# Modulation sums by transposes and ScalarE row sums in the first stage of a decoder layer

## The chip, the cores and the metric

The kernel runs on one NeuronCore of one Trainium2 chip. The metric is device time in microseconds for one execution of the whole program; before the change it is 685.23 us, the median of 3 runs (684.47 to 685.48).

## The reference, cut to what matters

One decoder layer over 512 tokens of width 1024. The part that the change touches is its beginning: the modulation vector from the condition `c`, the modulated RMSNorm and the first columns of the input projection.

```python
cs = jax.nn.silu(c)
mod = cs @ w_ada[l] + b_ada[l]
shift1, scale1, gate1, shift2, scale2, gate2 = [m[:, None, :] for m in jnp.split(mod, 6, axis=-1)]
h = _rmsnorm(x, norm1_g[l]) * (1.0 + scale1) + shift1
proj = h @ w_in[l]
qa, ka, va, qd, kd, vd, ga, gd = jnp.split(proj, points, axis=-1)
...
return _rmsnorm(x, final_g)
```

Behind it come sliding-window attention, differential attention, gates, an output projection and a gated MLP with a convolution; none of that is changed.

## The kernel before, in words

The first stage works on the 1024 channels in eight blocks of 128, k = 0 to 7. For each k it needs `mods[k]`, two numbers per channel: a scale (column 0) and a shift (column 1). With them ScalarE makes `hTh[k]`, the transposed, normalised and modulated activations (128 channels by 512 tokens), and a plain copy `hf`, from which VectorE makes the remainder `hTl[k]`: an fp32 operand is carried as a high and a low part, and a product takes three matrix products (high by high, high by low, low by high). The 768 columns of this stage's projection (queries, keys and values of the first branch) lie in six PSUM banks, `acc6`, which take the products of all eight k. `DONE = (0, 4, 2, 5, 1, 3)` (line 175) is the order of the banks; the sixth is bank 3.

TensorE's work on one k is written out in `mm_k` (line 396): part 0 is high by high and high by low over the banks, twelve products of 512 columns; part 2 is the six products with `hTl[k]`. In the loop over `gi` (line 484) the modulation sums of the next k stand between the two. They are made as follows.

- `ac_first` and `ac_ops` (lines 282 and 292): `w_ada`'s block for k (`adaw`, two halves, j = 0 for scale and 1 for shift) has 1024 rows, eight groups of 128. ScalarE multiplies two of the groups by silu(c), VectorE adds the other six (`scalar_tensor_tensor`, line 301) and folds the two partial sums into one tile `ac[k][0]` (line 302), 128 partitions by two times 128 columns. What is left is a sum over the 128 partitions.
- `reduce_mod` (line 317) makes that sum on TensorE: for each j a product of `ac` with one column of ones (line 328), which leaves 128 x 1 numbers in the PSUM tile `pa`.
- `finish_mod` (line 331): VectorE computes (pa + bsc1) * n1g into column 0 (line 334), ScalarE pa + bsh into column 1 (line 338).
- `h_turn` (line 376) transposes the next block of the normalised input, `xt`, four transposes; `h_tile` (line 381) is the two ScalarE passes to `hTh` and `hf` (line 384).

k = 0 and k = 1 have paths of their own (`direct0`, `early_mod`), which the change leaves alone. The order of VectorE, ScalarE and TensorE in this stage is that of the code (`manual_schedule`); the loads stand on SyncE's queue in the order `adaw`, `w0` for k = 0 to 7 (lines 243 to 250). Behind the loop a scheduler places the next stage's instructions, some of them among the last ones of this stage: the casts `w768_0_h` and `w1280_0_h` of the next stage's weights (line 128) on ScalarE, their remainders (line 129) on VectorE, and `pcv`, a small transpose of convolution constants (line 561), with its copy `cv` (line 563).

A step is named by its `gi` below: step gi multiplies block gi and prepares block gi + 1, so the changed steps are 1 to 6.

Of the kernel before, what the change touches and what calls it, by code (L numbers as in the profile page):

```python
# [8 lines left out]
F32 = mybir.dt.float32  # L9
F32R = mybir.dt.float32r  # L10
AF = mybir.ActivationFunctionType
ALU = mybir.AluOpType
PSUM = bass.MemoryType.PSUM

P = 128
# [45 lines left out]
def kernel(  # L61
# [22 lines left out]
    nc = tc.nc  # L84
# [3 lines left out]
    def pool(name, bufs=1, space=None, stack=ctx):  # L88
        kw = {} if space is None else {"space": space}
        return stack.enter_context(tc.tile_pool(name=name, bufs=bufs, reuse_waits="tile", **kw))  # L90

    cpool = pool("const")
# [13 lines left out]
    def tbank(name, shape=(P, S)):  # L106
        return bank("t", 2, list(shape), name)
# [34 lines left out]
    ones = cpool.tile([P, P], F32, name="ones")  # L142
    nc.gpsimd.memset(ones, 1.0)
    ident = cpool.tile([P, P], F32, name="ident")
# [31 lines left out]
    DONE = (0, 4, 2, 5, 1, 3)  # L176
# [42 lines left out]
    pp = pool("p1", stack=p1)  # L219
# [54 lines left out]
    cols = cpool.tile([P, NR], F32, name="cols")  # L274
    nc.vector.tensor_copy(cols, pc)
    bsh, bsc1, n1g, sublnc = cols[:, 0:8], cols[:, 8:16], cols[:, 16:24], cols[:, 24:25]
    nc.vector.tensor_scalar_add(bsc1, bsc1, 1.0)
    nc.vector.tensor_scalar_mul(n1g, n1g, -0.5)
    nc.vector.tensor_scalar_mul(sublnc, sublnc, -0.5 * (1.0 - LAM_INIT))
    ac, mods, wts = {}, {}, {}  # L280


    def ac_first(gi, b):
        a = pp.tile([P, 2, P], F32, tag=f"ac{b}", bufs=2, name=f"ac{gi}_{b}")
        aw = adaw[gi]
        if gi < ALONE and b:
            nc.vector.tensor_scalar_mul(a, aw[:, :, b], cs[:, b : b + 1])
        else:
            nc.scalar.activation(a, aw[:, :, b], AF.Copy, scale=cs[:, b : b + 1])
        ac.setdefault(gi, {})[b] = a  # L290

    def ac_ops(gi, low):
        aw = adaw[gi]
        if gi < ALONE:
            ac_first(gi, 1)
        order = (3, 2, 5, 4) if gi == 1 else (3, 5, 2, 7, 4, 6) if gi < ALONE else (3, 2, 5, 4, 7, 6)
        for n, kk in enumerate(order):
            if gi == 1 and n == 1:
                split_lo(0, 1)
            a = ac[gi][kk % 2]  # L300
            nc.vector.scalar_tensor_tensor(a, aw[:, :, kk], cs[:, kk : kk + 1], a, ALU.mult, ALU.add)
        nc.vector.tensor_add(ac[gi][0], ac[gi][0], ac[gi][1])
        low()

    def direct(pa, j, k, kks, start=True, stop=False):
        for kk in kks:
            nc.tensor.matmul(
                pa[:, j],
                adaw[k][:, j, kk],
                cs[:, kk : kk + 1].to_broadcast([P, P]),  # L310
                start=start and kk == kks[0],
                stop=stop and kk == kks[-1],
            )

    def early_mod(gi):
        pa = tbank(f"pa{gi}", (P, 2, P))
        direct(pa, 0, gi, (6, 7))
        return pa

    def reduce_mod(gi, early=None):  # L320
        pa = early or tbank(f"pa{gi}", (P, 2, P))
        for j in range(2):
            if early:
                if j:
                    direct(pa, 1, gi, (6, 7))
                nc.tensor.matmul(pa[:, j], ac[gi][0][:, j], ones, start=False, stop=True)
            else:
                nc.tensor.matmul(pa[:, j, 0:1], ac[gi][0][:, j], ones[:, 0:1], start=True, stop=True)
        return pa

    def finish_mod(k, pa):
        pa = pa if k == 0 else [pa[:, 0], pa[:, 1]]
        m = pp.tile([P, 16], F32, tag="mod", bufs=3, name=f"mod{k}")
        last = nc.vector.scalar_tensor_tensor(
            m[:, 0:1], pa[0][:, 0:1], bsc1[:, k : k + 1], n1g[:, k : k + 1], ALU.add, ALU.mult
        )
        if k:
            nc.scalar.activation(m[:, 1:2], pa[1][:, 0:1], AF.Identity, bias=bsh[:, k : k + 1])
        else:
            nc.vector.tensor_add(m[:, 1:2], pa[1][:, 0:1], bsh[:, k : k + 1])  # L340
        mods[k] = m
        return last

    def w0_views(k):
        wh, wl = wts[k]
# [9 lines left out]
    def split_hi(k, part=None):  # L355
        if part != 1:
            pl, nb = (wp, WB) if k % 2 == 0 else (pp, 2)
            wh = pl.tile([P, 768], F32R, tag="whi", bufs=nb, name=f"w0h{k}")
            wl = pl.tile([P, 768], F32R, tag="wlo", bufs=nb, name=f"w0l{k}")
            wts[k] = (wh, wl)  # L360
            rq, wq, lq = w0_views(k)
            nc.scalar.copy(wq, rq)
        if part != 0:
            nc.scalar.copy(wts[k][0][:, 512:768], w0[k][:, 512:768])

    def split_lo(k, part):
        wh, wl = wts[k]
        if part == 0:
            rq, wq, lq = w0_views(k)
            nc.vector.tensor_tensor(lq, rq, wq.bitcast(F32), ALU.subtract)  # L370
        else:
            nc.vector.tensor_sub(wl[:, 512:768], w0[k][:, 512:768], wh[:, 512:768].bitcast(F32))
# [3 lines left out]
    def h_turn(k):  # L376
        pts[k] = tbank(f"xt{k}")
        for t in range(NT):
            nc.tensor.transpose(pts[k][:, t * P : (t + 1) * P], xn[:, t, k * P : (k + 1) * P], ident)

    def h_tile(k, between=None):
        hf = pp.tile([P, S], F32, tag="hf", bufs=2, name=f"hf{k}")
        for dst in (hTh[k], hf):
            nc.scalar.activation(dst, pts[k], AF.Identity, bias=mods[k][:, 1:2], scale=mods[k][:, 0:1])
            if dst is not hf and between is not None:
                between()
            if dst is not hf and k + 1 < ALONE:
                ac_first(k + 1, 0)
        hfs[k] = hf

    def h_low(k):
        nc.vector.tensor_sub(hTl[k], hfs[k], hTh[k].bitcast(F32))

    FIRST = (0, 2, 1, 3, 4, 5)

    def mm_k(k, part, some=DONE):
        wh, wl = wts[k]
        last = k == KT - 1
        if part == (2 if last else 1):
            return  # L400
        for i in some:
            for p in (1, 2) if last and part else (0, 1) if part == 0 and not last else (part,):
                lhs, rhs = ((wh, hTh), (wl, hTh), (wh, hTl))[p]
                nc.tensor.matmul(
                    acc6[i], lhs[:, i * P : (i + 1) * P], rhs[k], start=k == 0 and p == 0, stop=last and p == 2
                )
# [28 lines left out]
    def scale_x(t):  # L435
        nc.scalar.activation(xn[:, t, HEAD:], xn[:, t, HEAD:], AF.Copy, scale=rst[:, t : t + 1])
# [37 lines left out]
    for j in range(2):  # L474
        nc.tensor.matmul(pa0[j], a0[j], ones, start=False, stop=True)
    turn(3)
    finish_mod(0, pa0)
    split_hi(0, 0)
    keep_warm(2)
# [3 lines left out]
    for gi in range(KT):  # L483
        more = gi + 1 < KT
        if more:
            if gi == 0:
                scale_x(2)
            split_hi(gi + 1)
            if gi == 1:
                scale_x(3)  # L490
            ac_ops(gi + 1, lambda: h_low(gi))
        else:
            h_low(gi)
            lp = cpool.tile([P, 2, 64], F32, name="lp")
            ls = cpool.tile([P, 2], F32, name="ls")
            nlam = cpool.tile([P, 1], F32, name="nlam")
            nc.vector.tensor_mul(lp, lamv[:, 0:4:2], lamv[:, 1:4:2])
            nc.vector.reduce_sum(ls, lp, axis=mybir.AxisListType.X)
            nc.scalar.activation(ls, ls, AF.Exp)
            nsink = cpool.tile([P, 8], F32, name="nsink")  # L500
            nc.vector.tensor_scalar_mul(nsink, sink, -1.0)
            nc.vector.tensor_sub(nlam, ls[:, 1:2], ls[:, 0:1])
            nc.vector.tensor_scalar_add(nlam, nlam, -LAM_INIT)
        if gi == 0:
            h_turn(1)
        mm_k(gi, 0, DONE if gi else FIRST[:5])
        mm_k(gi, 1)
        if more:
            if gi == 0:
                split_lo(1, 0)  # L510
            pa = reduce_mod(gi + 1, early_mod(1) if gi == 0 else None)
            if gi == 0:
                mm_k(0, 0, FIRST[5:])
            if ALONE <= gi + 2 < KT:
                ac_first(gi + 2, 1)
                ac_first(gi + 2, 0)
            if gi:
                h_turn(gi + 1)
            last_mod = finish_mod(gi + 1, pa)
            if gi:  # L520
                split_lo(gi + 1, 0)
            split_lo(gi + 1, 1)
            h_tile(gi + 1)
        mm_k(gi, 2)
# [503 lines left out]
    for i in range(SWA_PAIRS):  # L1028
        more = i + 1 < SWA_PAIRS
# [502 lines left out]
    last = range(KT - TAIL, KT)  # L1532
# [568 lines left out]
```

## Time and profile before

| what | value |
|---|---|
| median of 3 runs | 685.23 us |
| the profiled execution's own time | 685.38 us |
| its span, first to last instruction | 683.6 us |
| TensorE busy in the span | 673.7 us (99%) |
| VectorE, ScalarE, GpSimd busy | 562.5, 398.1, 98.4 us |
| granted TensorE clock | 0.997 |

Times in rows are microseconds from the start of the span, and the second number of a timeline row is how long the instruction took. PE is TensorE's products, PEld its weight loads, DVE VectorE, ACT ScalarE, POOL GpSimd, SP the load queue. Products are pipelined, so a product's share of the time is the distance to the next one's start, not its length. An `x4` behind a row counts instructions that were merged. Names of tiles lose their numbers in the trace: `pa` is the modulation sums of any k.

### The profile page before, as it was taken

Reading aid. Unit: us, or ns where it says so; the run is one execution under the profiler, and the core shown is the slowest. Engines: PE = TensorE matmul, PEld = TensorE weight load, DVE = VectorE, ACT = ScalarE, POOL = GpSimd, SP = SyncE. Lnnn points to the kernel's source line nnn. Section 1 sums busy time; section 2 is a strip of 40 time slices with the busy share of each in tenths; the row PEclk is TensorE's granted clock in tenths of the full one; section 3 lists DMA queues with packets and bytes.
Section 4 is the critical chain, followed back from the end, with each engine's and each line's share of the span. In section 5 each row is a group of like instructions: output and inputs, shape, how many; then the busy total and the mean of one; then the engine's idle time right before and its main releaser. Section 6 shows DMA issues by size and latency. Waiting matters only on the chain. (4 is left out here: it accounts for less than half of the span.)

```text
span 683.6 us, 10903 instructions
## 1 busy us (share of the span) xinstructions
PE 673.7 (99%) x4005; PEld 582.2 (85%) x4005; DVE 562.5 (82%) x1075; ACT 398.1 (58%) x722; POOL 98.4 (14%) x119
## 2 busy tenths in 40 slices
PE   8999999999999999999999999999999999999995
PEld 5887887878888888888899999999999998888885
DVE  4999875988796756794589988988888999979997
ACT  6776774546543223233377756666666776656765
POOL 3000000011022011021030101112111102440300
PEclk9999999999999999999999999999999999999998
DMA  9995422565466885469644788886879848995903
GB/s 304 351 301 175 144 62 65 161 167 163 142 159 179 254 245 164 163 187 340 204 89 108 174 195 206 185 184 190 213 163 217 207 146 203 201 204 144 167 1 123
DMA packets 117141, 123.87 MB, mean 181 GB/s; under 512 B 5063, under 2 KB 94184, under 8 KB 117088
## 3 DMA queue, kind: packets, MB, share of 16 engines
q1 hardware_dynamic: 97246, 95.11, 44.2%
q0 software_dynamic: 19648, 27.79, 24.3%
q8 instruction: 31, 0.51, 0.3%
q10 hardware_dynamic: 194, 0.28, 0.1%
q14 instruction: 22, 0.18, 0.1%
HBM read 118.97 MB, written 2.11 MB: 177 GB/s over the span
## 5 line engine op out<-in xcount | busy, mean ns | idle before, releaser
L1390 PE MATMUL up<-t,m_whi 128*128 128x256 f32 x512 | 93.5, 283 | 0.1
L1390 PEld LDWEIGHTS up<-t,m_whi 128*128 128x128 f32 x512 | 79.8, 192 | 0.8 <-ACT up L1427 0.3
L1390 PE MATMUL up<-t,m_wlo 128*128 128x256 f32 x256 | 72.4, 283 | 0.0
L953 POOL DMA_DIRECT2D arow<-arow x28 | 22.5, 802 | 249.1 <-DVE sd L822 123.2
L1390 PEld LDWEIGHTS up<-t,m_wlo 128*128 128x128 f32 x256 | 49.1, 192 | 0.0
L1373 PE MATMUL up<-bhl,p_whi 128*128 128x512 f32 x136 | 48.9, 399 | 0.0
L1272 POOL DMA_DIRECT2D s<-in_w_up_dram x21 | 26.9, 1352 | 144.2 <-DMA s<-in_w_up_dram 65.8
L1302 ACT CAST m_whi<-s 128x1024 fp32r<-128x1024 f32 x31 | 32.6, 1052 | 23.8 <-PE up L1390 10.3
L1306 DVE TENSOR_TENSOR m_wlo<-s,m_whi 128x1024 fp32r<-128x1024 f32 x31 | 37.9, 1221 | 6.0 <-ACT m_whi L1302 5.5
L945 DVE SCALAR_TENSOR_TENSOR arow<-ra,cs,arow 128x512 f32<-128x512 f32 x56 | 41.7, 747 | 0.6
L1377 PE MATMUL up<-bhl,p_wlo 128*128 128x256 f32 x136 | 38.3, 281 | 0.0
L1390 PE MATMUL up<-bhl,p_whi 128*128 128x256 f32 x192 | 35.1, 283 | 0.0
L1390 PE MATMUL up<-t,p_whi 128*128 128x256 f32 x176 | 32.1, 283 | 0.0
L1373 PEld LDWEIGHTS up<-bhl,p_whi 128*128 128x128 f32 x136 | 25.6, 188 | 5.5
L1390 PEld LDWEIGHTS up<-bhl,p_whi 128*128 128x128 f32 x192 | 30.0, 192 | 0.0
L817 ACT ACTIVATE sd<-sd,dmx 128x128 f32<-128x128 f32 (+3 forms) x32 | 17.7, 556 | 17.2 <-DVE dmx L807 17.2
L1390 PEld LDWEIGHTS up<-t,p_whi 128*128 128x128 f32 x176 | 27.4, 191 | 0.4
L1390 PE MATMUL up<-bhl,p_wlo 128*128 128x256 f32 x96 | 27.2, 283 | 0.0
L1377 PEld LDWEIGHTS up<-bhl,p_wlo 128*128 128x128 f32 x136 | 25.7, 189 | 0.0
L1390 PE MATMUL up<-t,p_wlo 128*128 128x256 f32 x88 | 24.9, 283 | 0.0
L1296 DVE TENSOR_TENSOR s<-s,wa 128x1024 f32<-128x1024 f32 x20 | 24.4, 1219 | 0.0
L1397 ACT ACTIVATE gT<-a,cv 128x512 f32<-128x512 f32 x22 | 17.8, 814 | 10.1 <-DVE a L1431 6.2
(501 smaller groups left out, 2085.6 us busy)
## 6 DMA issues: line engine op xcount, KB each, us to landing
ra<-in_w_ada_dram SPq DMA_DIRECT2D x32, 512.0 KB, 4.5
wa<-in_w_up_dram SPq DMA_DIRECT2D x22, 512.0 KB, 4.6
s<-in_w_up_dram SPq DMA_DIRECT2D x21, 512.0 KB, 5.6
s<-in_w_up_dram POOLq DMA_DIRECT2D x21, 512.0 KB, 7.3
w<-in_w_in_dram SPq DMA_DIRECT2D x12, 512.0 KB, 4.8
a<-in_w_up_dram SPq DMA_DIRECT2D x11, 512.0 KB, 4.2
b<-in_w_down_dram SPq DMA_DIRECT2D x10, 512.0 KB, 3.9
adaw<-in_w_ada_dram SPq DMA_DIRECT2D x8, 512.0 KB, 6.8
```

Source lines behind the costliest of these rows:

```text
L817: exp = nc.scalar.activation(pm[m], pm[m], AF.Exp, bias=mx[:, m : m + 1], scale=slope, accum_out=ls)
L945: nc.vector.scalar_tensor_tensor(ac, r[:, a], cc, ac, ALU.mult, ALU.add)
L953: nc.gpsimd.dma_start(whole[0:n], whole[n : 2 * n], accum_op=ALU.add)
L1272: nc.gpsimd.dma_start(dst, upblock(*blk), accum_op=ALU.add)
L1296: nc.vector.tensor_add(src, src, R[J, "a11" if name == "m6" else "a12"])
L1302: nc.scalar.copy(W[J, name][0], R[J, SRC[name]])
L1306: nc.vector.tensor_sub(lo, R[J, SRC[name]], hi.bitcast(F32))
L1373: nc.tensor.matmul(bk, wh[:, k, cu], bhl[:, i, k].rearrange("p b n -> p (b n)"), start=False, stop=k == 3, skip_group_check=True,)
L1377: nc.tensor.matmul(bk[:, :H], wl[:, k, cu], bhl[:, i, k, 0], start=False, stop=k == 3, skip_group_check=True)
L1390: nc.tensor.matmul(o[u], w[:, k, cu], b[:, k], start=opens and k == 0 and x == 0, stop=k == 3 and x == 2, skip_group_check=True,)
L1397: nc.scalar.activation(grow(j), av[J][:, u], AF.Identity, bias=cv[:, 66 + j : 67 + j], scale=cv[:, 44 + j : 45 + j])
```

## The change

For k from 2 on, `reduce_mod` no longer multiplies `ac` by ones. It transposes both halves on TensorE, 128 x 128 each, so that the numbers to be added lie along a row. `finish_mod` then reads `pa` on ScalarE alone: an Identity activation over 128 columns with `accum_out`, which writes the row's sum into the column of `mods[k]`; scale and bias are applied to every element, so the bias is a 128th of what it was. These shares are made once, in step 1, in a new tile `share`: a ScalarE pass over 128 x 16 numbers and a GpSimd multiplication of 128 x 8. VectorE has no part left in it. The elements themselves go to a tile `spread`, which nobody reads.

The transposes also stand elsewhere: from step 1 on the six banks' first twelve products are cut into five banks, then the modulation, then the sixth bank.

```diff
-                nc.tensor.matmul(pa[:, j, 0:1], ac[gi][0][:, j], ones[:, 0:1], start=True, stop=True)
+                nc.tensor.transpose(pa[:, j], ac[gi][0][:, j], ident)
...
-        last = nc.vector.scalar_tensor_tensor(
+        if k > 1:
+            for j, scale, bias in ((0, n1g[:, k : k + 1], share[:, 8 + k : 9 + k]), (1, 1.0, share[:, k : k + 1])):
+                spread = pp.tile([P, P], F32, tag="spread", name=f"spread{k}_{j}")
+                last = nc.scalar.activation(spread, pa[j], AF.Identity, bias=bias, scale=scale, accum_out=m[:, j : j + 1])
+            mods[k] = m
+            return last
+        nc.vector.scalar_tensor_tensor(
...
+                nc.scalar.activation(share, cols[:, 0:16], AF.Copy, scale=1.0 / P)
+                nc.gpsimd.tensor_tensor(share[:, 8:16], share[:, 8:16], n1g, ALU.mult)
...
-        mm_k(gi, 0, DONE if gi else FIRST[:5])
+        mm_k(gi, 0, DONE[:5] if gi and more else DONE if gi else FIRST[:5])
...
-            if gi == 0:
-                mm_k(0, 0, FIRST[5:])
+            mm_k(gi, 0, (DONE if gi else FIRST)[5:])
```

On TensorE in step 1, before the change (`a1` is the fifth bank's sum, `a3` the sixth's, `w0h1` and `w0l1` the weights' two parts):

```order
L404 MATMUL a1_114<-hTA_116,w0h1_293 128x512
L404 MATMUL a1_114<-hTA_116,w0l1_294 128x512
L404 MATMUL a3_115<-hTA_116,w0h1_293 128x512
L404 MATMUL a3_115<-hTA_116,w0l1_294 128x512
L328 MATMUL pa2_373<-ones_67,ac2_0_337 128x1 x2
L379 MATMUL xt2_380<-ident_69,xn_122 128x128 x4
L404 MATMUL a0_110<-hTA_116,w0h1_293 128x512
```

The same place with the change:

```order
L410 MATMUL a1_114<-hTA_116,w0h1_294 128x512
L410 MATMUL a1_114<-hTA_116,w0l1_295 128x512
L329 MATMUL pa2_374<-ident_69,ac2_0_338 128x128 x2
L410 MATMUL a3_115<-hTA_116,w0h1_294 128x512
L410 MATMUL a3_115<-hTA_116,w0l1_295 128x512
L385 MATMUL xt2_383<-ident_69,xn_122 128x128 x4
L410 MATMUL a0_110<-hTA_116,w0h1_294 128x512
```

The pair on `ac2` stands two products of 512 columns earlier and is a pair of transposes; it is no longer next to the transposes of `xt2`. The other five steps read the same.

On ScalarE around the last block's modulation, before (`mod7` is `mods[7]`, `hThB` the last two blocks of `hTh`, the two `w..._h` the next stage's weights):

```order
L364 CAST w0h7_599<-w0_7_175 128x256
L128 CAST w768_0_h_705<-w768_0_703 128x1024
L128 CAST w1280_0_h_711<-w1280_0_709 128x1024
L338 ACTIVATE mod7_631<-pa7_623,cols_196 128x1
L384 ACTIVATE hThB_117<-xt7_626,mod7_631 128x512
L384 ACTIVATE hf7_636<-xt7_626,mod7_631 128x512
```

With the change:

```order
L370 CAST w0h7_612<-w0_7_175 128x256
L338 ACTIVATE spread7_0_645,mod7_644<-pa7_634,share_201,cols_196 128x128
L338 ACTIVATE spread7_1_647,mod7_644<-pa7_634,share_201 128x128
L128 CAST w768_0_h_720<-w768_0_718 128x1024
L390 ACTIVATE hThB_117<-xt7_639,mod7_644 128x512
L390 ACTIVATE hf7_651<-xt7_639,mod7_644 128x512
L128 CAST w1280_0_h_726<-w1280_0_724 128x1024
```

The first cast of the next stage has moved from ahead of the modulation to between the modulation and `hThB`, the second one behind `hf7`.

On TensorE the small transpose `pcv` stood behind all products of block 7; now it stands ahead of them:

```order
L410 MATMUL a1_114<-hTlB_118,w0h6_560 128x512
L410 MATMUL a3_115<-hTlB_118,w0h6_560 128x512
L568 MATMUL pcv_709<-ident_69,crow_107 128x88
L410 MATMUL a0_110<-hThB_117,w0h7_612 128x512
L410 MATMUL a4_111<-hThB_117,w0h7_612 128x512
```

What moved is one narrow product past the 18 of block 7. On VectorE the six `mod` instructions of line 334 are gone, and the copy `cv` stands ahead of the last `hTl`. Behind the first stage no engine's order differs.

More of the change, by code (lines that the diff above doesn't have):

```diff
@@ L279 @@
     nc.vector.tensor_scalar_mul(sublnc, sublnc, -0.5 * (1.0 - LAM_INIT))
+    share = cpool.tile([P, 16], F32, name="share")
     ac, mods, wts = {}, {}, {}
@@ L341, in finish_mod @@
         mods[k] = m
-        return last
     def w0_views(k):
```

## The prediction, made before the changed kernel had run

> **What bounds the kernel now.** I read the page's busy shares first, then the stretches of the first stage, then the waits there, then one step of the timeline.
>
> ```profile
> PE 673.7 (99%) x4005; PEld 582.2 (85%) x4005; DVE 562.5 (82%) x1075; ACT 398.1 (58%) x722; POOL 98.4 (14%) x119
> ```
>
> ```profile
> 25.00:35.00 10.00, 10.00 (x55) 8.31 (x53) 9.27 (x23) 6.80 (x15) 0.00 (x0) 1.00 1.11 351
> 55.50:677.00 621.50, 620.69 (x3752) 541.23 (x3750) 516.38 (x950) 356.31 (x643) 92.27 (x94) 1.00 0.66 169
> ```
>
> Columns of the second fence: stretch, its length, busy time of PE, PEld, DVE, ACT and POOL, granted clock, DMA share, GB/s. TensorE is without a gap in the middle of the stage that changes, and idles 0.8 of the 621.5 us behind it. So TensorE time that goes here should be gone at the end, and so should TensorE time that is lost. DMA is full here (1.11 of 16 engines), which will matter: loads come when they come.
>
> ```profile
> ACT mod L338 <- DVE mod L334: 6.9, 7, 1.6
> PEld pa L328 <- DVE ac L302: 0.3, 1, 0.3
> ```
>
> These waits of 15 to 56 us (who waited for whom, us in total, times, longest) say that ScalarE has about 1 us to spare per step, and that TensorE's weight load waited for the modulation operand once. Step 3 in order of time, first TensorE, then ScalarE, which there waited 0.90 us for a load:
>
> ```profile
> 33.95 0.39 PE L404 MATMUL a<-hTA,w0l 128*128 128x512 f32 x1
> 34.18 0.50 PE L328 MATMUL pa<-ones,ac 128*128 128x1 f32 x4
> 34.54 0.63 PE L379 MATMUL xt<-ident,xn 128*128 128x128 f32 x4
> 34.93 1.86 PE L404 MATMUL a<-hTA,w0h 128*128 128x512 f32 x7
> 36.62 0.39 PE L404 MATMUL a<-hTA,w0l 128*128 128x512 f32 x1
> ```
>
> ```profile
> 33.42 0.91 ACT L289 ACTIVATE ac<-adaw,cs 128x256 f32<-128x256 f32 x2 [0.90 <-DMA adaw<-in_w_ada_dram]
> 35.27 0.78 ACT L384 ACTIVATE hTA<-xt,mod 128x512 fp32r<-128x512 f32 x1
> ```
>
> Seven products start between 34.93 and 36.62; the seventh, the first that needs the new hTA, starts one spacing of 0.23 us before 36.62, at 36.39. hTA ended at 35.27 + 0.78 = 36.05. The lead is 0.34 us, and nothing waited.
>
> **The price of a narrow product.** Two stretches behind the stage give it:
>
> ```profile
> 55.25 0.39 PE L404 MATMUL a<-hTlB,w0h 128*128 128x512 f32 x1
> 55.48 0.24 PE L561 MATMUL pcv<-ident,crow 88*128 88x88 f32 x1
> 55.51 0.48 PE L132 MATMUL pq<-hTA,w_h 128*128 128x512 f32 x1
> 55.82 0.39 PE L133 MATMUL pq<-hTA,w_h 128*128 128x512 f32 x1
> 61.04 0.39 PE L134 MATMUL pq<-hTA,w_l 128*128 128x512 f32 x1
> 61.27 0.60 PE L556 MATMUL pva<-ident,vaT 128*128 128x128 f32 x4
> 61.62 0.48 PE L132 MATMUL pq<-hTA,w_h 128*128 128x512 f32 x1
> 61.94 0.40 PE L133 MATMUL pq<-hTA,w_h 128*128 128x512 f32 x1
> ```
>
> From the last wide start before to the second wide start after, less the two wide spacings of 0.46: one narrow pass costs 55.82 - 55.25 - 0.46 = 0.11, four cost 61.94 - 61.04 - 0.46 = 0.44. So it is 0.11 a pass, however the passes are grouped, and cutting a stretch in two costs nothing extra. In step 3 the second wide start is 36.62 - 6 x 0.23 = 35.24, and 35.24 - 33.95 - 0.46 = 0.83 for eight passes. Why eight:
>
> ```profile
> L328 PE MATMUL pa<-ones,ac 128*128 128x1 f32 x24 | 3.1, 234 | 0.0
> L379 PE MATMUL xt<-ident,xn 128*128 128x128 f32 x28 | 4.4, 280 | 0.0
> ```
>
> Twelve fp32 products with ones are 24 records, two passes each; 28 transposes are 28 records. **Removed:** with the change a step has two and four passes, 0.22 + 0.44 = 0.66 instead of 0.83: 0.17 us less, six times, **-1.0 us**. At 0.11 for each of the eight it would be 0.22, so -1.3; I take the first, measured on the stretch itself. [...]
>
> **Step 1, the operand comes too late.** The transposes stand two wide products earlier, 0.46 us, and need `ac`:
>
> ```profile
> 23.39 0.39 PE L404 MATMUL a<-hTA,w0l 128*128 128x512 f32 x1
> 24.09 0.53 PE L328 MATMUL pa<-ones,ac 128*128 128x1 f32 x4
> 26.57 0.39 PE L404 MATMUL a<-hTA,w0l 128*128 128x512 f32 x1
> ```
>
> ```profile
> 23.46 0.43 DVE L302 TENSOR_TENSOR ac<-ac,ac 128x256 f32<-128x256 f32 x1
> 23.81 0.68 DVE L392 TENSOR_TENSOR hTA<-hf,hTA 128x512 fp32r<-128x512 f32 x1
> 25.14 0.69 DVE L370 TENSOR_TENSOR w0l<-w,w0h 128x512 fp32r<-128x512 f32 x1 [0.27 <-issue]
> 28.58 0.43 DVE L302 TENSOR_TENSOR ac<-ac,ac 128x256 f32<-128x256 f32 x1
> ```
>
> `ac` is ready at 23.46 + 0.43 = 23.89, nothing ahead of it on VectorE goes, and TensorE took it at 24.09. It would now take it in the slot 23.39 + 0.23 = 23.62. TensorE is in order, so the sixth bank stands behind it: **+0.47 us**, from 24.09 again.
>
> **Step 2** had 0.11 of such a wait: from L328 to L379 it is 34.54 - 34.18 = 0.36 in step 3, and 0.47 in step 2:
>
> ```profile
> 29.06 0.61 PE L328 MATMUL pa<-ones,ac 128*128 128x1 f32 x4
> 29.53 0.64 PE L379 MATMUL xt<-ident,xn 128*128 128x128 f32 x4
> ```
>
> VectorE need no longer wait for `pa`; its w0l can start behind the remainder at 23.81, some 0.6 after it, at 24.4 instead of 25.14, so step 2's `ac` comes at 29.01 - 0.7 = 28.3, before its slot of 28.60. **-0.11 us.** If the 0.27 of "issue" stays, it is 28.6, on the slot's edge. Later steps free VectorE further.
>
> **ScalarE's pair.** No row shows an accumulating read of `pa`; the nearest are those of the attention:
>
> ```profile
> 63.00 0.39 ACT L683 ACTIVATE st<-st,nm 128x128 f32<-128x128 f32 x1
> 63.29 0.18 ACT L683 ACTIVATION_READ_ACCUMULATOR st<-st,nm 128x1 f32 x1
> 63.38 0.50 ACT L683 ACTIVATE st<-st,nm 128x256 f32<-128x256 f32 x1
> ```
>
> 128 more columns cost 0.11. The first of the pair has scale and bias as tiles, as hTA has: 0.78 - 3 x 0.11 = 0.45; the second 0.39. The second waits for the first one's end (one `spread` tile), each read of the sum ends 0.08 behind its activation, and a hand-over takes 0.04: 0.45 + 0.08 + 0.04 + 0.39 + 0.08 + 0.04 = 1.08, and I take 1.05 from the pair's start to hTA's. Without any overlap of the reads it is 1.3.
>
> Step 1: `pa` complete at 24.09 + 0.11 + 0.28 = 24.48. ScalarE is later:
>
> ```profile
> 23.76 0.89 ACT L289 ACTIVATE ac<-adaw,cs 128x256 f32<-128x256 f32 x2
> ```
>
> The new share pass before `ac` costs at most the 0.29 of a 128-column pass, so the pair starts at about 24.85; GpSimd's small multiplication, bounded by 0.55 here, ends about then:
>
> ```profile
> 6.46 0.55 POOL L195 TENSOR_TENSOR r<-ms,mhalf 128x1 f32<-128x1 f32 x1 [1.88 <-DVE ms L191]
> ```
>
> hTA: 24.85 + 1.05 + 0.78 = 26.68. Its product's slot was 26.57 - 0.23 = 26.34 and is now 26.34 - 0.17 + 0.47 = 26.64. No row shows how little lead does (0.34 was never used up); with 0.1 to 0.2 the loss is **+0.2 us**.
>
> Steps 2 to 5: from the transposes' slot T, `pa` is there at T + 0.39, hTA ends at T + 0.42 + 1.05 + 0.78 = T + 2.25, and its product stands at T - 0.23 + 2 x 0.46 + 0.66 + 5 x 0.23 = T + 2.50. Lead 0.25: no loss, but not much cover. In step 3 the load decides: ScalarE is free at 33.42 + 0.91 = 34.33 whatever came before, hTA ends at 34.33 + 1.05 + 0.78 = 36.16, and the slot is then about 36.4: just covered.
>
> **Step 6, the cast in between.** Before, the casts filled ScalarE's idle time:
>
> ```profile
> 47.38 2.01 ACT L128 CAST w_h<-w 128x1024 fp32r<-128x1024 f32 x2
> ```
>
> ```profile
> 49.08 0.50 PE L328 MATMUL pa<-ones,ac 128*128 128x1 f32 x4
> 51.29 1.56 PE L404 MATMUL a<-hThB,w0h 128*128 128x512 f32 x6
> ```
>
> By the terms so far TensorE is -5 x 0.17 - 0.11 + 0.47 + 0.2 = -0.29 here: slot 49.08 - 0.46 - 0.29 = 48.33, pair from 48.75, cast from 49.7, hThB 0.95 behind that (two casts take 2.01, overlapped) at 50.65, done at 51.43. Its product would stand at 51.29 - 0.29 - 0.17 + 0.11 (pcv, moved ahead, returned later) = 50.94. With 0.1 of lead that is **+0.6 us**; the hTlB behind it stays covered by the six hThB products of 1.4 us. Between 0.4 and 0.7.
>
> **Sum:** -1.0 - 0.11 + 0.47 + 0.2 + 0.6 = +0.15 us; with the passes at -1.3, -0.15. Against the profiled execution's 685.38 us that is 685.2 to 685.5; this execution is 0.15 above the median of 685.23. I say **685.2 us**: the gain is spent in steps 1 and 6. The three runs before lie 1.0 us apart, so 0.2% (1.4 us: under 683.9 or over 686.6) is about what can be told from no change.
>
> **Rivals.**
>
> *Faster, the losses don't come* (a shorter pair, a cast that fits). Then -1.0 to -1.4 on paper, but the load of step 3 caps it: hTA not before 36.16, its product not before 36.26 against 36.39, at most -0.13 up to there, then -0.17 to -0.22 in each of three steps: -0.65 to -0.8, **684.6 us**. For it speaks ScalarE's 6.9 us of waiting; against it `ac` at 23.89, which the change doesn't touch. Over 0.2% needs the load earlier too. 15%, about 5% beyond 0.2%.
>
> [...] 4%.
>
> *Slower, ScalarE's chain sets the pace.* Steps 2 to 5 have a lead of 0.25. At 1.3 for the pair it is 0 and, with 0.1 to 0.2 needed, each step loses 0.1 to 0.2, step 6 as much more: +0.5 to +1.0, **686.0 us**. It is over 0.2% from a pair of about 1.45 on. For: the pair has two waits on its own engine that no row shows. Against: the overlapped rows at 63 us. 14%, about 8% beyond.
>
> *The change does nothing that is seen*, because TensorE's order is given and each step ends by its operand: 685.2 as forecast, for another reason; the leads above speak against. 5%.
>
> Forecast 62%. Range 684.3 to 686.2: the capped gain less a third of the runs' spread, and the slower rival. The scatter of the runs adds some 3% to the faster and 2% to the slower side. Faster by over 0.2% 0.09, within 0.81, slower 0.10.
>
> **What would show it.** Right: twelve transposes of `ac` in single records 0.11 apart; step 1's transposes at 24.1, not 23.6; steps 2 to 5 shorter by 0.17 to 0.3; pair to hTA near 1.05; TensorE waiting for hThB near 51. Wrong: transposes in two records or with a gap at each cut; a wait for hTA in every step; hThB before 51; TensorE's time behind 56 us changed by more than 0.3 us.

## The result, and the profile after

The changed kernel takes 691.93 us (median of 6 runs, 691.36 to 695.52), the kernel before 685.28 us (6 runs, 684.43 to 686.12): a ratio of 1.0113, 95% interval 1.0099 to 1.0127. The forecast was 685.2. The profiled execution of the changed kernel took 691.67 us, its span is 689.9 us.

The busy times of the page first:

```profile
PE 675.0 (98%) x3993; PEld 580.4 (84%) x3993; DVE 561.3 (81%) x1069; ACT 402.8 (58%) x741; POOL 99.8 (14%) x120
```

TensorE has 12 records fewer, as foretold; VectorE has 6 fewer, and ScalarE is busy 4.7 us longer. The two stretches that the prediction read, in the changed kernel:

```profile
25.00:35.00 10.00, 9.51 (x47) 7.57 (x48) 9.69 (x23) 8.74 (x22) 0.42 (x1) 1.00 1.13 316
55.50:677.00 621.50, 619.36 (x3729) 538.64 (x3728) 513.38 (x938) 355.46 (x640) 93.20 (x94) 1.00 0.67 169
```

TensorE now has a gap in the first stage, idles 2.1 us behind it instead of 0.8, and the loads come at 316 GB/s instead of 351 with much the same busy share of the DMA engines (1.13, before 1.11). That last column is the finding: the transfers got slower, and no instruction of the change issues one. The waits of the first stage (15 to 60 us):

```profile
ACT ac L290 <- DMA adaw<-in_w_ada_dram: 3.6, 4, 2.4
PE a L410 <- ACT hTA L390: 1.4, 1, 1.4
PE pa L329 <- DVE ac L303: 0.7, 1, 0.7
PE a L410 <- ACT hThB L390: 0.4, 1, 0.4
```

and those of TensorE between 225 and 350 us, where the kernel before has none:

```profile
PE pgd L132 <- DVE ta L991: 1.4, 1, 1.4
PE pB L134 <- DVE wbd L129: 0.5, 1, 0.5
```

Starts of the same TensorE products in both traces give the account: the changed kernel is 0.9 us late at 18.6 us, before any changed instruction has run, 1.0 at the start of step 1 (19.4 us), 1.7 at step 1's transposes of `xt` (24.5), 3.4 at the end of the stage (51.3 us), 4.8 at 242 us, 5.5 at 298, 6.2 at 343, and stays there. So about half is lost up to the end of the first stage, 1.0 us of it ahead of the change, and half far behind it.

Step 3 of the changed kernel, ScalarE and then TensorE:

```profile
36.77 0.91 ACT L290 ACTIVATE ac<-adaw,cs 128x256 f32<-128x256 f32 x2 [2.42 <-DMA adaw<-in_w_ada_dram]
37.59 0.44 ACT L338 ACTIVATE spread<-pa,share,cols 128x128 f32<-128x128 f32 x1
37.93 0.19 ACT L338 ACTIVATION_READ_ACCUMULATOR spread<-pa,share,cols 128x1 f32 x1
38.15 0.37 ACT L338 ACTIVATE spread<-pa,share 128x128 f32<-128x128 f32 x1
38.64 0.78 ACT L390 ACTIVATE hTA<-xt,mod 128x512 fp32r<-128x512 f32 x1
```

```profile
36.47 1.65 PE L410 MATMUL a<-hTA,w0h 128*128 128x512 f32 x6
39.48 0.50 PE L410 MATMUL a<-hTA,w0h 128*128 128x512 f32 x1 [1.36 <-ACT hTA L390]
```

The pair takes 38.64 - 37.59 = 1.05 us, the very figure of the prediction. But the load that frees ScalarE lands at 36.70 us; in the kernel before the same load landed at 33.40.

Why the transfers are slower: `share` takes 64 bytes of each partition, in the middle of a pool, and every tile allocated behind it moved up by 64 bytes. In the kernel before the tiles that the loads write (`adaw`, the weights, the inputs) begin at multiples of 512 bytes; in the changed kernel at 64 past one. (This is read from the program's allocations; the traces hold no addresses.)

### The profile page after: what moved, and what is told of

It is laid out like the page before. It is cut to its first block, busy times and chain, and to the rows that moved or that the text cites. A ratio compares the mean times of both kernels' runs of the same rounds, so it can differ in the third digit from the quotient of the medians.

```text
span 689.9 us, 10895 instructions
## 1 busy us (share of the span) xinstructions
PE 675.0 (98%) x3993; PEld 580.4 (84%) x3993; DVE 561.3 (81%) x1069; ACT 402.8 (58%) x741; POOL 99.8 (14%) x120
## 5 line engine op out<-in xcount | busy, mean ns | idle before, releaser
L1279 POOL DMA_DIRECT2D s<-in_w_up_dram x21 | 27.2, 1367 | 144.3 <-DMA s<-in_w_up_dram 64.5
L1309 ACT CAST m_whi<-s 128x1024 fp32r<-128x1024 f32 x31 | 32.6, 1052 | 23.8 <-PE up L1397 10.3
L1397 PEld LDWEIGHTS up<-t,p_whi 128*128 128x128 f32 x176 | 27.4, 191 | 0.4
L1397 PE MATMUL up<-bhl,p_wlo 128*128 128x256 f32 x96 | 27.2, 283 | 0.0
L410 PE MATMUL a<-hTA,w0h 128*128 128x512 f32 x72 | 24.3, 411 | 1.5 <-ACT hTA L390 1.4
```

The costliest lines, as they stand in the source:

```text
L410: nc.tensor.matmul(acc6[i], lhs[:, i * P : (i + 1) * P], rhs[k], start=k == 0 and p == 0, stop=last and p == 2)
L1279: nc.gpsimd.dma_start(dst, upblock(*blk), accum_op=ALU.add)
L1309: nc.scalar.copy(W[J, name][0], R[J, SRC[name]])
L1397: nc.tensor.matmul(o[u], w[:, k, cu], b[:, k], start=opens and k == 0 and x == 0, stop=k == 3 and x == 2, skip_group_check=True,)
```

## Experiments

The theory after the traces: the 64 bytes cost the time (P). The rival: the changed instructions cost it (I). Each group of kernels was timed beside the kernel before (medians 685.42, 684.93, 685.46 and 685.41 us); differences below are to the median of the same group, unless said otherwise.

### Placement: four kernels

The changed kernel with only the tile's size edited:

```diff
-    share = cpool.tile([P, 16], F32, name="share")
+    share = cpool.tile([P, P], F32, name="share")[:, 0:16]
```

> The changed kernel with all its instructions in the same order, but the tile share takes 512 bytes of a partition in place of 64 (its first 16 columns are used), so that every later tile begins again at a multiple of 512 bytes, as before the change. Theory P (placement: the 64 bytes moved the destinations of the loads, and late loads cost the 6.6 us): 685.3 us, 684.6 to 686.0, and the loads' 512-byte packets back at 27.4 ns. Rival I (instructions: the pair on ScalarE, the cast in step 6 and the transposes' place cost it): 691.9 us, as the changed kernel.

Measured: 686.52 us (12 runs, 684.95 to 693.55), ratio 1.0028 (1.0006 to 1.0050).

And the kernel before with an unused tile at the same place, of 64, 256 and 128 bytes. The 256 bytes are to tell two forms of P apart: in its 256-byte form a start off a multiple of 256 bytes costs time, so that this pad costs nothing; in its 512-byte form a start off a multiple of 512 does, so that it costs as much as 64 bytes.

```diff
+    pad = cpool.tile([P, 16], F32, name="pad")
+    nc.gpsimd.memset(pad, 0.0)
     ac, mods, wts = {}, {}, {}
```

> The kernel before, with an unused tile of 64 bytes where the changed kernel has share (one small GpSimd fill of it is the only new instruction). Theory P: 691 us, 690 to 692.5, 512-byte packets at about 31 ns, adaw of step 3 some 3 us later. Rival I: 685.3 us, no change.

> As the run before with 256 bytes: tells by which step the placement counts. [...] Theory P in a 512-byte form: 691 us. Rival I: 685.3 us.

> As the run before with 128 bytes. Theory P, 256-byte form or 512-byte form: 691 us, 690 to 692.5. If only what is off 128 bytes counts: 685.3 us. Rival I: 685.3 us.

Measured: 64 bytes 687.46 us (687.33 to 688.17), ratio 1.0029 (1.0018 to 1.0041); 256 bytes 685.22 us, ratio 0.9995 (0.9987 to 1.0004); 128 bytes 687.94 us (687.60 to 688.18), ratio 1.0034 (1.0022 to 1.0047).

The transfers of the first 50 us say the same. Packets, volume and mean rate, one fence each for the kernel before and the pads of 256, 64 and 128 bytes:

```profile
DMA packets 22399, 15.96 MB, mean 319 GB/s; under 512 B 849, under 2 KB 20633, under 8 KB 22395
```

```profile
DMA packets 22998, 16.29 MB, mean 326 GB/s; under 512 B 854, under 2 KB 21215, under 8 KB 22994
```

```profile
DMA packets 20967, 14.88 MB, mean 298 GB/s; under 512 B 813, under 2 KB 19428, under 8 KB 20964
```

```profile
DMA packets 21091, 14.94 MB, mean 299 GB/s; under 512 B 816, under 2 KB 19552, under 8 KB 21088
```

The mean time of a 512-byte packet in these 50 us, counted from the packets' records, is 27.4 ns in the kernel before, 27.2 at 256 bytes, 31.1 at 64, 31.5 at 128, 31.2 in the changed kernel and 27.3 in that with `share` on 512 bytes. So an unused tile of 64 bytes makes the tuned kernel 2.0 us slower, and one of 256 bytes costs nothing. By the packet 64 bytes cost 14% and 128 bytes 15%; the pad of 128 makes the kernel 2.5 us slower. So the 256-byte form of P is the one that agrees. What a transfer does with a start off such a multiple no trace shows.

But P fell short of its numbers: I had expected 691 from the pad of 64, and 685.3 from `share` on 512 bytes. 2.0 and 1.1 us do not add up to 6.65, and two runs of the 512-byte kernel took over 691 us. Something else adds to it.

### TensorE's instruction count

What the traces of the two kernels with the change (691.67 and 688.36 us) have in common, and those without it don't, stands on GpSimd's queue. Behind 190 us the program sums a modulation row of a later gate over the partitions by seven transfers, each of which adds one half of a tile to the other (`arow`, line 960 in the changed kernel), one after another; then the row goes out (`mod_rows`) and comes back to all partitions (`g1b`, `xn`), and VectorE waits for it. The last of them in the kernel before, and in the changed kernel:

```profile
194.75 0.82 POOL L953 DMA_DIRECT2D arow<-arow  x1 [18.33 <-DVE dls L820]
...
221.31 0.79 POOL L953 DMA_DIRECT2D arow<-arow  x1 [1.85 <-DMA arow<-arow]
224.08 0.52 POOL L956 DMA_DIRECT2D mod_rows<-arow  x1 [1.98 <-DMA arow<-arow]
```

```profile
197.97 0.83 POOL L960 DMA_DIRECT2D arow<-arow  x1 [18.27 <-DVE dls L827]
...
228.08 0.79 POOL L960 DMA_DIRECT2D arow<-arow  x1 [2.87 <-DMA arow<-arow]
233.79 0.52 POOL L963 DMA_DIRECT2D mod_rows<-arow  x1 [4.92 <-DMA arow<-arow]
```

29.3 us from the first addition to `mod_rows` became 35.8, and VectorE's wait for the result went from 2.5 to 8.9 us. The wait in the kernel before, and in the changed kernel:

```profile
DVE g1b L1177 <- DMA xn<-in_b_ada_dram: 2.5, 1, 2.5
```

```profile
DVE g1b L1184 <- DMA xn<-in_b_ada_dram: 8.9, 1, 8.9
```

Behind it VectorE's `ta` and `wbd` are late, for which TensorE waits in the rows at 225 to 350 us above. Nothing in the program differs there, and the pad of 64 bytes, which moves the same tiles, has no such delay (table below). What differs from it is when the packets of an instruction queue arrive. One of the two instruction queues in the page's table, the same before and after, is this:

```profile
q8 instruction: 31, 0.51, 0.3%
```

By the packets' records it brings 16,384 bytes at a time, in 0.9 to 1.6 us, once for some 250 of TensorE's products and weight loads (31 packets, 4005 of each in the kernel before, 3993 in the changed one). From this I take it for the fetch of TensorE's code. With 12 products and 12 weight loads fewer the packet that came at 190.2 us now comes at 198.2, in the first addition (195.7 in the 512-byte kernel, whose additions start at 195.5).

Theory F: the moved fetch starts the delay. To test it the 24 instructions were put back at a place where TensorE waits anyway:

```diff
-            m = min(n, 4)
+            m = min(n, piece)
...
-    keep_warm(WARM_FIRST)
+    keep_warm(WARM_FIRST, 1)
```

and likewise for `WARM_EARLY` and `keep_warm(2)`: the warming products are cut into pieces of 128 columns.

> The changed kernel with share on 512 bytes, and 24 more TensorE instructions at the start, where TensorE waits for the first loads (three of the warming products are cut into pieces of 128 columns: six more fp32 products of two passes, each pass a weight load and a product), so that TensorE's 16 KB instruction fetches fall as before the change: near 26.3 and 190 us in place of 27.3 and 195.7. Theory F (a fetch that moved: the one at 195.7 us meets the first of the eight serial halving transfers, which then runs into the next loads, VectorE waits for its end near 240 us): no TensorE wait near 240 and 300 us, 685.3 to 686.2 in nearly all runs, spread under 2 us. Rival C (chance, or another trace of the change): 686.5 median with some runs of 688 to 693, as without the 24. For the load of step 3, which landed 0.64 us late with share on 512 bytes: 33.4 us if the fetch at 27.3 was the cause, 34.0 if not.

> The changed kernel with share on its 64 bytes and the same 24 TensorE instructions more at the start. Theory F: only placement (2.0 us, as the pad of 64 bytes) and the first stage's terms (0.2 to 0.8 us) are left: 687.5 to 688.5, spread under 2 us. Rival C: 691.9 with a spread of 4 us, as the changed kernel.

> One part of the change alone, on the kernel before: the twelve fp32 products with ones of line 328 are transposes, in their old place, and VectorE and ScalarE finish as before from one column of pa, so the sum over the rows of ac is left out. No share, no pair on ScalarE, no product moved; 12 records of products and 12 weight loads fewer on TensorE. Theory F: the fetches fall at 27 and 195 us, the load of step 3 lands 0.6 us later, and some runs lose 1 to 7 us behind 195 us: median 685 to 687 with a spread of over 3 us. Rival C: six times 0.16 us less and nothing behind: 684.3, capped by the load of step 3 at 684.6, spread as before.

Measured: on 512 bytes 685.93 us (11 runs, 685.21 to 688.13), ratio 1.0018 (1.0009 to 1.0026); on 64 bytes 688.82 us (688.62 to 689.76), ratio 1.0060 (1.0048 to 1.0072); the transposes alone (where the sum is left out) 686.84 us with the widest spread of the three, 683.25 to 690.38 (ratio 1.0024, 1.0003 to 1.0045). So the count is worth some 3 us on 64 bytes; on 512 bytes the intervals with and without the 24 overlap. And taking 24 instructions away brings scatter to the kernel before without ScalarE's pair and without `share`. Parts of F failed: the spread on 512 bytes is 2.9 us, where under 2 was foretold; the first-stage fetch came at 21 us, not at 26.3 as I had put it, and the load of step 3 landed at 33.0 us on 512 bytes, but no earlier on 64 (36.80).

Three more kernels, and a control, ask whether it is the fetch and the chain. Half the instructions; the additions of that one row cut short, which leaves its sum out; and the 24 instructions put in behind the first stage:

```diff
-                nc.gpsimd.dma_start(whole[0:n], whole[n : 2 * n], accum_op=ALU.add)
+                few = 1 if idx == 1 else n
+                nc.gpsimd.dma_start(whole[0:few], whole[n : n + few], accum_op=ALU.add)
```

> The changed kernel with share on its 64 bytes and 12 more TensorE instructions at the start (three of the warming products cut off as pieces) in place of 24. TensorE's fetch near 198 us should stand about 1.3 us earlier, at 196.9, right ahead of the first halving transfer (198.0 us) instead of in it. Theory F, if only a fetch inside the chain's first transfers costs: 688.8 as with 24, spread under 2 us. If the order of the transfers ahead of the chain counts too: between, 689 to 691.5. Rival C (not the place of the fetch): 691.9 with a spread of 4 us.

> The changed kernel, share on its 64 bytes, TensorE's instructions as they are, but the seven halving transfers of the second of the four gate rows (line 960, from 198 us) add one row each instead of 64, 32, ... rows, so that this row's sum is left out; the number of transfers and their place in the program stay. Theory F (the chain's late end is what TensorE pays near 245 and 300 us): the chain ends before 225 us in place of 239, no TensorE wait for VectorE near 245 us, 688.5 to 689.7, at most what the later rows' chains still lose. Rival (the later loss has another carrier, VectorE's or ScalarE's own work): 691.9 and the wait near 245 us stays.

> The changed kernel, share on its 64 bytes, the first stage untouched; instead twelve 512-column products of the next stage (the first two units' middle high-by-high products, 57 to 75 us) are cut into two of 256 columns, which gives TensorE the 24 instructions behind the first stage. Theory F (the place of the fetch that meets the second gate row's halvings): the fetch at 198 us goes to about 194, and the time to 688.5 to 689.8 in most runs. Rival S (not the fetch: the pieces at the start of the other runs shifted the first stage's loads): 691.9, and the TensorE wait near 245 us stays.

> A control: the kernel before with the 24 TensorE instructions more at the start and nothing else. Theory F: the fetch at 190 us goes to about 186, further from the halvings that start at 194.8: 685.3, at most 0.5 less. Rival S (pieces at the start help by themselves): 684.5 or less. If it becomes slower by 0.5 or more, the places of other fetches count as well.

Measured: 12 instructions 689.00 us (688.43 to 689.61, one run at 693.92), ratio 1.0060 (1.0036 to 1.0083); the short chain 689.30 us (688.65 to 691.09), ratio 1.0057 (1.0040 to 1.0074); 24 instructions behind the first stage 689.52 us (688.39 to 692.45), ratio 1.0066 (1.0047 to 1.0084); the control 685.65 us, ratio 1.0008 (0.9999 to 1.0016). None of the three traces has a TensorE wait for VectorE near 245 us, and pieces at the start do not help the kernel before. Rivals C (chance) and S (the pieces at the start help by themselves) fall. But two fetches did not come where F put them: 194.2 us with 12 put back instead of 196.9, and 190.8 in the control instead of 186. The traces side by side, from the start of the first addition to the landing of `xn`:

| kernel | fetch, against the first addition's start | length of the chain |
|---|---|---|
| changed | +0.2 us | 44.6 us |
| share on 512 bytes | +0.3 | 43.9 |
| transposes alone (a run of 684.80) | +0.4 | 38.0 |
| 64 bytes, 24 put back | -4.1 | 38.7 |
| 64 bytes, 12 put back | -3.6 | 39.1 |
| 64 bytes, 24 behind the first stage | -4.4 | 38.7 |
| 512 bytes, 24 put back | -4.4 | 40.3 |
| pad of 64 bytes | -4.4 | 39.1 |
| before | -4.5 | 38.2 |

Wherever the fetch falls ahead of the chain, the chain takes 38 to 40 us; where it falls into the first addition, it takes 44 in two traces and 38 in one, and these three kernels' times scatter by 4.2, 8.6 and 7.1 us, where that of the kernel before scatters by 1.7 to 3.7. The scatter alone doesn't separate them: it is 5.5 us with 12 put back (one run at 693.92) and 4.1 with the 24 behind the first stage. That the count decides on 64 bytes, and that the chain carries the loss, is shown. That it is the fetched packet itself which holds up the chain is not: the first addition took 7.8 us in the changed kernel, but with 512 bytes it took 6.4 with the fetch in it and 6.5 with 24 put back and the fetch long over, so there the longer chain arose in later additions.

### The first stage's own terms

With 24 put back, 64 bytes still cost 688.82 - 684.93 = 3.9 us, 1.9 more than the pad of 64 alone. In the traces TensorE ends the first stage 3.5 us late there and 2.1 with the pad, 1.4 more, and step 3 has all of it. ScalarE with the pad of 64 bytes in the kernel before:

```profile
36.25 0.91 ACT L291 ACTIVATE ac<-adaw,cs 128x256 f32<-128x256 f32 x2 [2.25 <-DMA adaw<-in_w_ada_dram]
37.06 0.24 ACT L340 ACTIVATE mod<-pa,cols 128x1 f32<-128x1 f32 x1
37.34 0.78 ACT L386 ACTIVATE hTA<-xt,mod 128x512 fp32r<-128x512 f32 x1
```

From `ac` to `hTA` it is 1.09 us there and 1.87 in the changed kernel (36.77 to 38.64): behind a late load the pair's 0.8 us more is paid in full. The other 0.6 is the load, which lands later still with the change (36.80 us, and 36.70 in the changed kernel, against 36.22). Why is open; the place of the fetches in the first 40 us doesn't order the landings. So is the 0.5 us by which the medians differ more than these traces.

The last run makes two repairs on the kernel with 512 bytes and 24 put back:

```diff
-            last_mod = finish_mod(gi + 1, pa)
+            finish_mod(gi + 1, pa)
...
-            h_tile(gi + 1)
+            last_h = h_tile(gi + 1)
...
-    with tc.issue_after(last_mod.ins):
+    with tc.issue_after(last_h.ins):
```

where `h_tile` now returns its last activation, and the two lines that compute `share` stand in the prologue.

> The changed kernel with share on 512 bytes and the 24 TensorE instructions more, as in an earlier run (685.93), and two repairs: the first two casts of the next stage are issued behind the last block's hThB and hf instead of behind its modulation, and share is computed right after cols in the prologue, not on ScalarE ahead of ac in step 1. By the prediction's terms: TensorE's loss at hThB in step 6 falls from 0.60 to 0.1 us, that at hTA in step 1 from 0.54 to 0.35; 0.6 to 0.7 us less, 685.2, which would be the kernel before within 0.2%. Rival: the casts are now late for the next stage's first products or hTlB, and the 0.5 us comes back there: 685.9. For a version faster than the kernel before by over 0.2% nothing speaks.

Measured: 685.72 us (12 runs, 684.72 to 688.87), ratio 1.0014 (0.9999 to 1.0029), not to be told from the kernel before, nor from 685.93. Step 6 without the repair, and with it:

```profile
49.16 1.63 PE L410 MATMUL a<-hTlB,w0h 128*128 128x512 f32 x6
50.63 0.24 PE L568 MATMUL pcv<-ident,crow 88*128 88x88 f32 x1
51.25 1.66 PE L410 MATMUL a<-hThB,w0h 128*128 128x512 f32 x6 [0.38 <-ACT hThB L390]
```

```profile
50.71 1.56 PE L413 MATMUL a<-hThB,w0h 128*128 128x512 f32 x6
...
54.91 0.24 PE L569 MATMUL pcv<-ident,crow 88*128 88x88 f32 x1
55.57 0.50 PE L132 MATMUL pq<-hTA,w_h 128*128 128x512 f32 x1 [0.42 <-DVE qa L549]
```

The wait for `hThB` is gone, and 0.42 us of it comes back at the next stage's first product, which waits for VectorE's `qa`: the remainders of both cast weights, 1.22 us each, now stand between `hTlB` and `qa` on VectorE, where one of them stood ahead of `hTlB`. The rival was right in size and place, by way of VectorE. No version here beats the kernel before.

## Why the prediction was wrong

It forecast no change and the kernel became 1.1% slower. By parts: 2.0 us from placement, 1.9 from the pair behind the late load and from that load's own delay (1.4 of it in the traces), 2.8 from the chain of additions (6.65 less the 3.9 that are left with the count put back).

- **The step that failed** is the sentence "DMA is full here (1.11 of 16 engines), which will matter: loads come when they come". It saw the bound and then took every landing time from the trace of before, since the change issues no load: ScalarE was to be free at 34.33 us in step 3 "whatever came before". The address that a transfer writes to changes its time (27.4 ns a packet became 31.2), and the new tile moved the targets of these loads. The load of step 3 came 3.3 us later, and TensorE, "just covered" in the prediction, waited 1.36 us.
- **Its second hole** is "So TensorE time that goes here should be gone at the end, and so should TensorE time that is lost": the 0.8 us of idle time behind 56 us were taken as fixed. It named TensorE's time behind 56 us as a sign of error, and that sign showed: 2.8 us are lost there.
- **The rivals** all lay in the first stage's instructions. The slower one, ScalarE's chain, named the right engine for the 0.8 us of step 3, but a price of 1.45 for the pair as the point from which it decides. The pair cost 1.05; the load decided.
- **The passes** were right: twelve records, the pair of transposes at two passes (35.88 - 35.20 - 0.46 = 0.22 us in step 3 of the changed kernel), and with 512 bytes TensorE gains 0.16 us in each undisturbed step (0.45, 0.28, 0.13 us late at the transposes of `xt` in steps 4 to 6), foretold 0.17.
- **Step 1's operand**: the transposes started 0.29 us behind their slot on 512 bytes (23.81 instead of 23.52), foretold 0.47; VectorE's `ac` came 0.2 earlier than the prediction allowed. The wait for `hTA` there was 0.2 us, as foretold, plus 0.16 for TensorE's start behind it, which was not.
- **Step 6's cast**: 0.6 us, as foretold, by the mechanism foretold; the repair showed it.
- **The sum**: on 512 bytes the stage ends 0.72 us late instead of 0.15, and nearly all of the difference is the wait of 0.43 us in step 3 and the 0.1 us that the first product behind each wait took more (0.34 to the next start instead of 0.23). With the 24 instructions put back the trace ends the stage 0.04 us early, but there the load of step 3 landed at 33.0 us, 0.4 earlier than before, which is luck (it lands between 32.6 and 34.0 us in the seven traces whose tiles begin at multiples of 256 bytes), and the median of that kernel is still 1.0 us above the kernel before. So as a sum over instructions it stood within some 0.6 us; the case was decided by what the new tile's size and the number of instructions moved.

## What to carry to other kernels

Before costing an edit, ask what it moves without touching: a new tile shifts every tile behind it, and where loads set the pace a shift that is no multiple of 256 bytes can cost more than the edit is worth (64 and 128 bytes cost 2.0 and 2.5 us here, 256 nothing), so give a small tile a multiple of 256 bytes, or (not tried here) put it behind the load targets. Adding or taking away instructions can move later instruction fetches (with 24 fewer here one came at 198.2 instead of 190.2 us); where a chain of small dependent transfers ends just in time, test the edit with the count put back before you judge it. And where an engine waits for loads, take landing times as a range and ask what stands behind the load on that engine's queue.

## What the hardware showed that was not expected

- A 512-byte packet into SBUF took 27.2 to 27.4 ns from a multiple of 256 bytes and 30.4 to 31.5 ns from 64 or 128 past one; 2.0 to 2.5 us of 685 for the kernel before.
- In two traces a wait of under 2 us was followed by half of TensorE's clock. In the profiled run of the short chain (691.09 us) TensorE waited 1.74 us in step 3, and then:

```profile
40.01 0.50 PE L410 MATMUL a<-hTA,w0h 128*128 128x512 f32 x1 [1.74 <-ACT hTA L390]
```

```profile
40.00:41.50 1.50, 1.50 (x6) 1.24 (x7) 1.47 (x4) 1.44 (x3) 0.00 (x0) 1.00 1.09 344
41.50:44.90 3.40, 3.40 (x11) 2.59 (x10) 3.32 (x9) 1.89 (x6) 0.00 (x0) 0.50 1.12 311
44.90:46.00 1.10, 1.10 (x8) 0.95 (x7) 0.38 (x1) 0.62 (x2) 0.00 (x0) 1.00 0.84 186
```

The granted clock is 0.50 for 3.4 us, with products 0.43 us apart instead of 0.23, and TensorE falls back by another 1.6 us: from 40.01 to the product behind the next transposes of `xt`, at 45.06, it is 5.05 us, in the changed kernel 3.43 (39.48 to 42.91). A wait of 1.86 us did the same in the kernel with 24 instructions behind the first stage; waits of 1.36 and 1.59 us in the same place did not. Idle time alone doesn't decide: between 5 and 20 us TensorE was busy 12.60 of the 15 us in the kernel with 24 put back on 64 bytes, at a granted clock of 0.89, and 11.77 with the pad of 64 bytes, at 1.00. Whether it lies behind single runs of 692 to 695 us, which have no trace, is open: their mean granted clock is 0.994 to 0.996 in the changed kernel, where its profiled run has 0.998, but a run of 691.65 has 0.994 too, and the run of 693.92 has 0.998.
- The read of ScalarE's accumulated sum is a record of 0.19 us that adds 0.09 behind its activation; the pair with both reads took 1.05 to 1.08 us to the next activation.
